# Where the latent queries and keys of an attention layer are split into two parts: at each load, or once where they are made

## The chip, the cores and the metric

The kernel runs on one core of one Trainium2 chip. The metric is the device time of one execution in microseconds (us). A core has a matrix engine (PE, with its weight loads shown as PEld), a vector engine (DVE), a scalar engine (ACT), a third elementwise engine (POOL) and a queue engine (SP) that issues most transfers between on-chip memory and DRAM. Each engine works through its own instructions in order.

## The reference, cut to what matters

Two layers of a decoder trunk with 1024 tokens of width 1024. The change touches the first layer's latent attention: eight heads, each with a query and key of 64 elements made from a normalised low-rank vector, and 32 rotary elements; the rotary part of the key is shared by all heads.

```python
q = (rmsnorm(z_cq, q_norm) @ w_uq).reshape(b, s, MLA_HEADS, MLA_NOPE + MLA_ROPE)
q_nope = q[..., :MLA_NOPE]
q_rope = apply_rope(q[..., MLA_NOPE:], cos_r, sin_r)
kv = (rmsnorm(z_ckv, kv_norm) @ w_ukv).reshape(b, s, MLA_HEADS, MLA_NOPE + MLA_V)
k_nope = kv[..., :MLA_NOPE]
k_rope = apply_rope(z_kr[:, :, None, :], cos_r, sin_r)[:, :, 0, :]
...
s = jnp.einsum('bqhd,bkhd->bhqk', qn, k_nope) + jnp.einsum('bqhr,bkr->bhqk', qr, k_rope)
s = jnp.where(causal_block_mask(blk, seq), s.astype(jnp.float32) * scale, NEG_INF)
p = jax.nn.softmax(s, axis=-1).astype(v.dtype)
return jnp.einsum('bhqk,bkhd->bqhd', p, v)
```

## The kernel before, in words

Everything is held with features on the 128 partitions and tokens along the free dimension, in two chunks of C = 512 tokens. To keep precision, each matrix operand is held as two tiles of a reduced float format: `hi`, a rounded copy, and `lo`, what is left. `split` (line 89) makes them: ACT copies the source to `hi` (L91), DVE or POOL subtracts to get `lo` (L92). A product is three matmuls: hi by hi, hi by lo, lo by hi (L127, L128 and L130 in projections, L441 in scores).

The work of the first layer comes in stages.

1. The first projections, and a list of "first" jobs built in `even_first` (line 660). It ends with the jobs that the change touches: `kr` makes the rotary key of a chunk and stores it to the DRAM tensor `krd` (L693); `qrope` evicts the two halves of the rotary query (L702), rotates them (L707 to L712) and stores them to `qrd` (L713, L714); `v` evicts latent values (ACT, L726); and `to` evicts latent queries and keys, four pairs of heads by query and key by chunk, with a multiplication on DVE (L720) and stores them to `qd` and `kd` (L721). All evicted blocks go to tiles with the tag `t`, a ring of eight tiles of 128 by 512. The latent vectors that these jobs read lie in the ring of twenty `qk` tiles, which they fill entirely.
2. Beside these jobs, `ada_behind` (line 312) loads modulation weights (L281) and sums them on DVE (L283), a step at a time.
3. Latent attention in `latent_items` (line 769), with window attention joined in towards its end. For each head and chunk `load_latent` (line 750) is called one head and chunk ahead. It issues five transfers on SP (L763) into one of two wide tiles of tag `x8` (the profile calls it `x`): 64 rows of query, two lots of 16 rows of rotary query, 64 rows of key and 32 of rotary key. Then it splits query and key into four tiles of the `qk` ring. This happens sixteen times.
4. `weave` (line 1124) merges attention with a filling of further projections, which need weights from the `wr` ring (loads L107, splits on ACT and POOL) and stores their results; its merge by costs gives the order in which the program is written. A planner then fixes each engine's order before the run, by that order as priority and by its own estimates of when inputs and free tiles are there. A tile that is not free makes the instruction that would write it wait, and with it what stands behind it on its engine.

SP issues its transfers in order: weights, modulation weights, stores, loads of the attention, and the small transfers that turn softmax sums into rows (L479, L491).

Of the kernel before, what the change touches and what calls it, by code (L numbers as in the profile page):

```python
# [10 lines left out]
F32 = mybir.dt.float32  # L11
F32R = mybir.dt.float32r
# [10 lines left out]
C = 512  # L23
# [10 lines left out]
class Trunk:  # L34
# [4 lines left out]
    def __init__(self, ctx, tc, I, out):  # L39
        self.tc, self.nc, self.I, self.out = tc, tc.nc, I, out  # L40
        self.ctx = ctx
        self.sb = ctx.enter_context(tc.tile_pool(name="sb", bufs=1))
        self.ps = ctx.enter_context(tc.tile_pool(name="ps", bufs=1, space=PSUM))
        self.dr = ctx.enter_context(tc.tile_pool(name="dr", bufs=1, space=DRAM))
        self.sb2 = None
        self.BUFS = dict(self.BUFS)
        self.n = 0
        d = lambda name, shape: self.dr.tile(shape, F32, name=name, tag=name)
        self.x1d = d("x1d", [2, 128, 8, C])
        self.ogd = d("ogd", [2, 8, 2, 128, C])  # L50
        self.gd = d("gd", [8, 2, 128, C])
        self.qd = d("qd", [4, 128, 1024])
        self.qrd = d("qrd", [2, 128, 1024])
        self.kd = d("kd", [4, 128, 1024])
        self.krd = d("krd", [32, 1024])
        self.vd = d("vd", [5, 2, 128, C])
        self.wd = d("wd", [5, 2, 128, C])
        self.fd = d("fd", [8, 1024])
        self.rd = d("rd", [2, 8, 2, 2, C])
# [600 lines left out]
    def even_first(self, h, tables):  # L660

        nc, I = self.nc, self.I
# [4 lines left out]
        def keep(i, n, g, dst, rs, col=None):  # L667
# [13 lines left out]
                    return lambda: rs.__setitem__(ch, self.copied(self.rstd(sq[n, ch], 128 * n, col and col[:, 4 * ch:4 * ch + 4]), self.t("g", [128, C])))  # L681
            return use

        def kr(ch, p):
            cs = slice(ch * C, ch * C + C)
            a, b, mk = self.tmp(), self.tmp(), self.tmp()
            nc.sync.dma_start(mk, I["mk"][:, cs])
            nc.vector.tensor_tensor(out=a, in0=p, in1=mk, op=ALU.mult)
            nc.sync.dma_start(b[0:64], a[64:128])
            nc.gpsimd.tensor_tensor(out=a[0:64], in0=a[0:64], in1=b[0:64], op=ALU.add)  # L690
            nc.sync.dma_start(mk[0:32], a[32:64])
            nc.gpsimd.tensor_tensor(out=a[0:32], in0=a[0:32], in1=mk[0:32], op=ALU.add)
            nc.sync.dma_start(self.krd[:, cs], a[0:32])  # L693

        half = {}

        def qrope(w):
            def use(ch, p):
                mc, ms = tables
                cs = slice(ch * C, ch * C + C)  # L700
                t = self.tmp()
                nc.vector.tensor_tensor(out=t, in0=p, in1=rq[ch], op=ALU.mult)  # L702
                half[w, ch] = t
                if w == 1:
                    za, zb = half[0, ch], t
                    t0, t1 = self.tmp(), self.tmp()
                    nc.vector.tensor_tensor(out=t0, in0=za, in1=ms[:, cs], op=ALU.mult)  # L707
                    nc.gpsimd.tensor_tensor(out=t1, in0=zb, in1=ms[:, cs], op=ALU.mult)
                    nc.vector.tensor_tensor(out=za, in0=za, in1=mc[:, cs], op=ALU.mult)
                    nc.gpsimd.tensor_tensor(out=zb, in0=zb, in1=mc[:, cs], op=ALU.mult)  # L710
                    nc.vector.tensor_tensor(out=za, in0=za, in1=t1, op=ALU.subtract)
                    nc.vector.tensor_tensor(out=zb, in0=zb, in1=t0, op=ALU.add)  # L712
                    nc.sync.dma_start(self.qrd[0, :, cs], za)  # L713
                    nc.sync.dma_start(self.qrd[1, :, cs], zb)  # L714
            return use

        def to(d, r):
            def use(ch, p):
                z = self.tmp()
                nc.vector.tensor_tensor(out=z, in0=p, in1=r[ch], op=ALU.mult)  # L720
                nc.sync.dma_start(d[:, ch * C:ch * C + C], z)  # L721
            return use

        def v(ch, p, b):
# [6 lines left out]
        hh = {0: h[0], 1: h[1]}  # L731
        full = lambda n, use: (w[n], 8, 128, [(0, 8, hh, use)])
        jobs = [full(10 + i, keep(i, 3, self.v_qn, cn, rq)) for i in range(3)]
        jobs += [full(13 + i, keep(i, 2, self.v_kvn, kn, rk, rkc)) for i in range(2)]
        jobs += [self.gate_job(h, 15, 0), (I["wkr"], 8, 128, [(0, 8, hh, kr)]), self.gate_job(h, 16, 1)]
        cc, kk = {0: cn[0], 1: cn[1]}, {0: kn[0], 1: kn[1]}
        jobs += [(I["wqr"], 6, 128, [(3 * i, 3, cc, qrope(i)) for i in range(2)])]
# [12 lines left out]
    def load_latent(self, u, hh, c):  # L750

        nc = self.nc
        hd = 2 * u + hh
        cs = slice(c * C, c * C + C)
        out = []
        both = self.t("x8", [128, 1024])
        for n, parts in enumerate(([(0, 64, self.qd[u, 64 * hh:64 * hh + 64, cs])] +
                      [(64 + 16 * e, 80 + 16 * e, self.qrd[e, 16 * hd:16 * hd + 16, cs]) for e in range(2)],
                      [(0, 64, self.kd[u, 64 * hh:64 * hh + 64, cs]), (64, 96, self.krd[:, cs])])):
            raw = both[:, n * C:n * C + C]  # L760
            hi, lo = (t[:96] for t in self.hl("qk"))
            for a, b, d in parts:
                nc.sync.dma_start(raw[a:b], d)  # L763
            self.split(hi, lo, raw[:96])
            out.append((hi, lo))
        (qh, ql), (kh, kl) = out
        return (qh, ql, qh), (kh, kh, kl)

# [673 lines left out]
```

## Time and profile before

| what | value |
|---|---|
| median of three runs | 1367.68 us (1365.36 to 1367.77) |
| the profiled execution | 1368.67 us, of which the span of instructions is 1366.9 us |
| PE busy | 1269.7 us (93%) |
| DVE busy | 912.3 us (67%) |
| ACT busy | 734.4 us (54%) |
| POOL busy | 352.5 us (26%) |
| transfers | 173.85 MB, 127 GB/s over the span |
| clock granted to PE | 0.987 of full speed over the span |

Busy time is from one profiled execution; matmuls are pipelined, so a matmul of 512 columns that is shown with 0.39 us starts 0.23 us after the one before it where nothing holds it up. In rows of the order of time the first number is the start in us, the second the duration, and a bracket at the end holds the engine's idle time before it and what ended it. Rows by tile give the least, median and greatest duration in ns. Tile names stand without their numbers, and `out<-in` says what is written from what.

### The profile page before, as it was taken

The numbers are of one execution on the slowest core, as the hardware profiler recorded it, in microseconds if no ns is written. First come the engines' busy times: TensorE is split into PE (matmuls) and PEld (weight loads), VectorE is DVE, ScalarE is ACT, GpSimd is POOL, SyncE is SP. The second block draws the span as 40 slices with busy tenths as digits, with TensorE's granted clock in tenths as the row PEclk, the third lists the DMA queues.
The fourth block names the chain that finished last, engine by engine and source line by source line (L and its number), as shares of the span: only waits on it lengthen the run. The fifth ranks groups of instructions, "written<-read, shape, count | busy, mean of one in ns | idle before, by whom it ended". The sixth has DMA issues, their size and how long they took to land.

```text
span 1366.9 us, 20727 instructions
## 1 busy us (share of the span) xinstructions
PE 1269.7 (93%) x6876; PEld 1055.4 (77%) x6876; DVE 912.3 (67%) x2058; ACT 734.4 (54%) x1515; POOL 352.5 (26%) x324
## 2 busy tenths in 40 slices
PE   2899999999999999999979999999999999999996
PEld 1678778888777777777757878787888888887896
DVE  6855757777668785787866776667646564656475
ACT  4253226555558577765545554447545455556542
POOL 2243421331233215300003322321222212233400
PEclk9999999999999999999999999999999999999998
DMA  8606685555354444373533222212112121233283
GB/s 284 249 19 210 194 277 189 170 161 178 109 158 138 156 124 138 103 231 123 176 92 104 70 59 66 49 56 76 52 38 78 54 78 55 85 117 103 78 270 121
DMA packets 103723, 173.85 MB, mean 127 GB/s; under 512 B 16304, under 2 KB 25520, under 8 KB 103616
## 3 DMA queue, kind: packets, MB, share of 16 engines
q1 hardware_dynamic: 99104, 169.91, 38.9%
q10 hardware_dynamic: 4512, 2.62, 0.6%
q8 instruction: 54, 0.88, 0.3%
q14 instruction: 53, 0.43, 0.1%
HBM read 129.36 MB, written 31.72 MB: 118 GB/s over the span
## 4 chain that ended last, share of the span: by engine, by line
PE 42%; DVE 12%; ACT 6%; issue 5%; DMA 5%; POOL 1%; SPq 1%; POOLq 0%; DVEq 0%; ACTq 0%
PE pj L127 8%; PE pj L128 8%; PE pj L130 8%; PE S L441 6%; PE pt L501 3%; PE o L511 2%; DVE pt_l L92 1%; DVE p L463 1%; DMA wr<-in_wout_dram 1%; PE o L510 1%; ACT wh L91 1%; PE S L127 1%; PE S L130 1%; PE S L128 1%; DMA t<-wd 1%
## 5 line engine op out<-in xcount | busy, mean ns | idle before, releaser
L127 PE MATMUL pj<-h,wh 128*128 128x512 f32 (+1 forms) x816 | 338.9, 416 | 1.5 <-ACT wh L91 1.5
L128 PE MATMUL pj<-h,wh 128*128 128x512 f32 (+1 forms) x816 | 322.2, 395 | 0.0
L130 PE MATMUL pj<-h,wl 128*128 128x512 f32 (+1 forms) x800 | 316.0, 395 | 2.2 <-DVE wl L92 2.2
L92 POOL TENSOR_TENSOR wl<-wr,wh 128x512 fp32r<-128x512 f32 x126 | 166.4, 1330 | 461.5 <-ACT wh L91 428.9
L466 ACT ACTIVATE p<-p,sm 128x128 f32<-128x128 f32 (+3 forms) x192 | 148.8, 775 | 146.8 <-DVE sm L463 143.0
L92 DVE TENSOR_TENSOR pt_l<-pt,pt_h 128x512 fp32r<-128x512 f32 (+1 forms) x232 | 146.9, 635 | 99.4 <-ACT pt_h L91 97.5
L441 PE MATMUL S<-qk,qk 96*128 96x512 f32 (+5 forms) x720 | 175.3, 344 | 20.6 <-DVE sm L463 11.4
L130 PEld LDWEIGHTS pj<-h,wl 128*128 128x128 f32 x800 | 151.0, 189 | 35.0 <-DVE wl L92 3.8
L91 ACT ACTIVATE pt_h<-pt 128x512 fp32r<-128x512 f32 (+1 forms) x232 | 127.6, 552 | 89.3 <-PE pt L501 87.5
L127 PEld LDWEIGHTS pj<-h,wh 128*128 128x128 f32 (+1 forms) x816 | 153.9, 189 | 20.3 <-ACT wh L91 2.3
L441 PEld LDWEIGHTS S<-qk,qk 128*128 128x128 f32 (+1 forms) x720 | 120.2, 188 | 63.2 <-DVE sm L463 25.5
L128 PEld LDWEIGHTS pj<-h,wh 128*128 128x128 f32 (+1 forms) x816 | 154.4, 189 | 17.1 <-DVE h L92 0.2
L91 ACT ACTIVATE wh<-wr 128x512 fp32r<-128x512 f32 x165 | 100.9, 622 | 115.4 <-PE S L128 38.6
L501 PE MATMUL pt<-ident,p 128*128 128x128 f32 x840 | 134.3, 274 | 3.1 <-DVE p L945 3.1
L501 PEld LDWEIGHTS pt<-ident,p 128*128 128x128 f32 x840 | 101.5, 140 | 26.1 <-DVE p L945 4.4
L463 DVE CUSTOM_DVE_ANT_0 p<-S,mask 128x640 f32<-128x640 f32 (+7 forms) x128 | 96.0, 750 | 35.0 <-PE S L441 34.1
L510 PE MATMUL o<-pt_h,v 128*128 128x256 f32 (+1 forms) x408 | 106.3, 279 | 2.1 <-ACT pt_h L91 1.7
L511 PE MATMUL o<-pt_l,v 128*128 128x256 f32 (+1 forms) x408 | 102.3, 285 | 5.6 <-DVE pt_l L92 5.3
L348 POOL TENSOR_TENSOR t<-t,rs 128x512 f32<-128x512 f32 x26 | 36.8, 1414 | 229.0 <-DMA t<-t 147.4
L511 PEld LDWEIGHTS o<-pt_l,v 128*128 128x128 f32 x408 | 77.2, 189 | 16.6 <-DVE pt_l L92 11.2
L510 PEld LDWEIGHTS o<-pt_h,v 128*128 128x128 f32 x408 | 77.0, 189 | 11.2 <-ACT pt_h L91 4.8
L127 PE MATMUL S<-h,wh 128*128 128x512 f32 (+1 forms) x144 | 57.5, 399 | 3.9 <-ACT h L332 2.7
(317 smaller groups left out, 2288.6 us busy)
## 6 DMA issues: line engine op xcount, KB each, us to landing
wr<-in_wod_dram SPq DMA_DIRECT2D x80, 256.0 KB
wr<-in_wout_dram SPq DMA_DIRECT2D x68, 256.0 KB
ad<-in_wadab_dram SPq DMA_DIRECT2D x41, 256.0 KB
wr<-in_wev_dram SPq DMA_DIRECT2D x38, 256.0 KB
raw<-in_wadaa_dram SPq DMA_DIRECT2D x32, 256.0 KB
ogd<-t SPq DMA_DIRECT2D x32, 256.0 KB
t<-t SPq DMA_DIRECT2D x106, 64.0 KB
t<-rd SPq DMA_DIRECT2D x48, 128.0 KB
```

Of the source, the lines that this page charges most:

```text
L91: nc.scalar.activation(hi, src, AF.Copy)
L92: (lo_eng or nc.vector).tensor_tensor(out=lo, in0=src, in1=hi.bitcast(F32), op=ALU.subtract)
L127: nc.tensor.matmul(p, w[0][:, k, :m], h[0], start=first, stop=False)
L128: nc.tensor.matmul(p, w[0][:, k, :m], h[1], start=False, stop=last and w[1] is None)
L130: nc.tensor.matmul(p, w[1][:, k, :m], h[0], start=False, stop=last)
L348: nc.gpsimd.tensor_tensor(out=s, in0=s, in1=self.rs[:, cs], op=ALU.mult)
L441: nc.tensor.matmul(dst, a, k[:, s], start=(n == 0), stop=n == len(q) - 1)
L463: nc.vector.tensor_tensor_reduce(out=P[:, s], in0=S[:, s], in1=a, scale=-scale, scalar=init, op0=ALU.add, op1=ALU.min, accum_out=nm)
L466: nc.scalar.activation(P[:, :n], P[:, :n], AF.Exp, bias=nm, scale=-1.0, accum_out=l)
L501: nc.tensor.transpose(pt[:, n * 128:n * 128 + 128], b, self.ident)
L510: nc.tensor.matmul(o[:, qcols], w, hi[:, cols], start=start, stop=False)
L511: nc.tensor.matmul(o[:, qcols], w, lo[:, cols], start=False, stop=stop)
```

## The change

Each latent query and key block is split where it has just been made. `keep_split` takes a new `t` tile for `hi`, writes `lo` over the block itself, and stores both, so the four DRAM tensors get a dimension of two. `load_latent` no longer uses the `x8` tile and splits nothing: for `hi` and `lo` of query and key it issues ten transfers straight into the four `qk` tiles.

```diff
-        self.qd = d("qd", [4, 128, 1024])
-        self.qrd = d("qrd", [2, 128, 1024])
-        self.kd = d("kd", [4, 128, 1024])
-        self.krd = d("krd", [32, 1024])
+        self.qd = d("qd", [4, 2, 128, 1024])
+        self.qrd = d("qrd", [2, 2, 128, 1024])
+        self.kd = d("kd", [4, 2, 128, 1024])
+        self.krd = d("krd", [2, 32, 1024])
...
+        def keep_split(z, d, cs):
+            hi = self.t("t", [128, C], F32R)[:z.shape[0]]
+            lo = z.bitcast(F32R)
+            self.split(hi, lo, z)
+            for n, x in enumerate((hi, lo)):
+                nc.sync.dma_start(d[n, :, cs], x.bitcast(F32))
...
-            nc.sync.dma_start(self.krd[:, cs], a[0:32])
+            keep_split(a[0:32], self.krd, cs)
...
-                    nc.sync.dma_start(self.qrd[0, :, cs], za)
-                    nc.sync.dma_start(self.qrd[1, :, cs], zb)
+                    keep_split(za, self.qrd[0], cs)
+                    keep_split(zb, self.qrd[1], cs)
...
                 nc.vector.tensor_tensor(out=z, in0=p, in1=r[ch], op=ALU.mult)
-                nc.sync.dma_start(d[:, ch * C:ch * C + C], z)
+                keep_split(z, d, slice(ch * C, ch * C + C))
...
-        both = self.t("x8", [128, 1024])
-        for n, parts in enumerate(([(0, 64, self.qd[u, 64 * hh:64 * hh + 64, cs])] +
-                      [(64 + 16 * e, 80 + 16 * e, self.qrd[e, 16 * hd:16 * hd + 16, cs]) for e in range(2)],
-                      [(0, 64, self.kd[u, 64 * hh:64 * hh + 64, cs]), (64, 96, self.krd[:, cs])])):
-            raw = both[:, n * C:n * C + C]
-            hi, lo = (t[:96] for t in self.hl("qk"))
-            for a, b, d in parts:
-                nc.sync.dma_start(raw[a:b], d)
-            self.split(hi, lo, raw[:96])
-            out.append((hi, lo))
+        for parts in ([(0, 64, self.qd[u, :, 64 * hh:64 * hh + 64, cs])] +
+                      [(64 + 16 * e, 80 + 16 * e, self.qrd[e, :, 16 * hd:16 * hd + 16, cs]) for e in range(2)],
+                      [(0, 64, self.kd[u, :, 64 * hh:64 * hh + 64, cs]), (64, 96, self.krd[:, :, cs])]):
+            both = tuple(t[:96] for t in self.hl("qk"))
+            for n, t in enumerate(both):
+                for a, b, d in parts:
+                    nc.sync.dma_start(t[a:b].bitcast(F32), d[n])
+            out.append(both)
```

## The prediction

> **What bounds the kernel now.** I read the page first: its shares of busy time, then the slices.
>
> ```profile
> PE 1269.7 (93%) x6876; PEld 1055.4 (77%) x6876; DVE 912.3 (67%) x2058; ACT 734.4 (54%) x1515; POOL 352.5 (26%) x324
> ```
>
> PE is the bound over the whole span: 97 of 1366.9 us are left as gaps. The change touches two stages: the projections that make latent queries and keys, and the latent attention that reads them back. So the table by stretches comes next; its columns are PE, PEld, DVE, ACT and POOL busy time with the number of instructions, the clock, the DMA share and GB/s.
>
> ```profile
> 150.00:174.00 24.00, 21.63 (x97) 17.28 (x96) 18.37 (x23) 5.32 (x9) 10.61 (x8) 1.00 0.62 195
> 174.00:202.00 28.00, 26.86 (x123) 21.72 (x121) 16.98 (x27) 6.29 (x12) 4.88 (x4) 1.00 0.83 274
> 202.00:350.00 148.00, 144.43 (x818) 121.24 (x818) 106.67 (x212) 91.22 (x194) 38.66 (x45) 1.00 0.56 176
> 350.00:460.00 110.00, 103.67 (x604) 86.30 (x603) 79.79 (x185) 68.54 (x167) 33.80 (x35) 1.00 0.42 131
> 175.00:180.00 5.00, 3.85 (x17) 2.84 (x16) 3.25 (x5) 0.61 (x2) 1.45 (x2) 1.00 1.06 333
> ```
>
> From 150 to 174 us rotary queries and latent values are made, from 174 to 202 us the sixteen blocks of latent queries and keys (PE 96% busy, DMA 0.83 busy), and from 202 us on attention runs with projections as filling. In attention PE idles 148 - 144.4 = 3.6 us before 350 us and 110 - 103.7 = 6.3 us up to 460 us: 9.9 us is the most that lighter DVE and ACT can give back to PE's gaps there. The last row, the busiest five microseconds of DMA in this stage, gives the most that was moved, 333 GB/s.
>
> What ends PE's gaps in attention is in the view of the waits, for 202 to 460 us:
>
> ```profile
> PE S L441 <- DVE sm L463: 4.2, 7, 1.2
> PE o L511 <- DVE pt_l L92: 3.1, 4, 1.4
> ```
>
> DVE ends most of them, so DVE work taken out of attention is worth something. In the projections the gaps have two other makers, seen in the order of time:
>
> ```profile
> 162.59 0.69 ACT L726 ACTIVATE t<-S,rkc 128x512 f32<-128x512 f32 x1 [8.52 <-DVE t L712]
> 163.33 0.50 PE L140 MATMUL S<-wh,qk 128*128 128x512 f32 x1 [2.37 <-ACT t L726]
> 178.10 0.75 DVE L283 SCALAR_TENSOR_TENSOR ad<-ad,sc 128x512 f32<-128x512 f32 x1 [0.75 <-DMA ad<-in_wadab_dram]
> 178.77 0.68 DVE L720 TENSOR_TENSOR t<-S,g 128x512 f32<-128x512 f32 x1
> 179.51 0.50 PE L127 MATMUL S<-qk,p 128*128 128x512 f32 x1 [1.15 <-DVE t L720]
> ```
>
> At 162.6 us ACT had waited 8.5 us for one of the eight "t" tiles, and PE lost 2.4 us behind it. At 178 us DVE, in order, waited for a landing of the modulation weights (L283); the eviction L720 stood behind it, and PE lost 1.15 us. Both the "t" tiles and the landings are what the change asks more of.
>
> **The change part by part.** Rows for the prices (duration is least, median and most, in ns; the row of a stretch is here of instructions on "qk" tiles alone, where DVE's and ACT's are the four splits):
>
> ```profile
> L91 ACT ACTIVATE qk<-x x32: 615/622/634, 195.5 to 450.5; 96x512 fp32r<-96x512 f32 x32
> L92 DVE TENSOR_TENSOR qk<-x,qk x32: 675/687/1517, 196.1 to 452.3; 96x512 fp32r<-96x512 f32 x32
> L763 SPq DMA_DIRECT2D x<-qd x16: 450/451/590, 185.0 to 352.0; - x16
> L763 SPq DMA_DIRECT2D x<-qrd x32: 307/504/1579, 170.1 to 354.5; - x32
> L763 SPq DMA_DIRECT2D x<-krd x16: 303/582/1552, 165.7 to 359.1; - x16
> L721 SPq DMA_DIRECT2D qd<-t x8: 319/367/790, 176.0 to 201.3; - x8
> 174.00:202.00 28.00, 26.21 (x114) 20.75 (x112) 2.65 (x4) 2.53 (x4) 0.00 (x0) 1.00 0.83 274
> L92 DVE TENSOR_TENSOR qk<-x,qk 96x512 fp32r<-96x512 f32 x23 | 18.2, 794 | 3.8 <-ACT qk L91 3.8
> 450.32 1.43 DVE qk L92
> 452.42 0.73 DVE qk L92
> 418.64 0.74 DVE qk L92
> 395.81 3.32 DMA t<-wd
> L283 DVE SCALAR_TENSOR_TENSOR ad<-ad,sc 128x512 f32<-128x512 f32 x6 | 4.5, 752 | 4.8 <-DMA ad<-in_wadab_dram 4.2 <-ACT ad L286 0.6
> ```
>
> *Removed from the attention loads:* 32 ACT copies of 0.622 us (19.9 us) and 32 DVE subtracts of 0.687 us median (22 us, somewhat more by the slow ones). From 202 to 350 us that is 18.2 of DVE's 106.7 us, a sixth. PE's gaps there are 3.6 us, so a sixth is 0.6 us and all of them the upper end. In the next stretch three of the subtracts stand on the chain that ended last, 1.43 + 0.73 + 0.74 = 2.9 us. Gain taken: 0.6 + 2.9 = 3.5 us; bounds 0 (what follows on the chain is as late) and 9.9 us.
>
> *Added where queries and keys are made:* 22 copies and 22 subtracts (16 blocks from L720, four rotary query halves, two rotary keys), priced by the same rows at 13.7 us of ACT and 15.1 us of DVE. The two rotary key blocks fall near 140 us:
>
> ```profile
> 140.68 0.34 SPq L693 DMA_DIRECT2D krd<-t  x1
> 140.00:145.00 5.00, 4.62 (x22) 3.53 (x21) 3.33 (x4) 0.60 (x1) 1.93 (x2) 1.00 0.57 142
> ```
>
> PE has 0.4 us of gaps there, DVE and ACT have room, and nobody reads the rotary key before attention; taken at 0, at most 2 x 1.31 = 2.6 us if that cover were gone.
>
> *150 to 174 us:* four copies and four subtracts, 2.75 us more on a DVE that is busy 18.4 of 24 us, and four more "t" tiles in the ring that already kept ACT and PE waiting. Bounds 0 (the released tile of L712 comes ahead of the new work) and 2.75 us (all subtracts ahead of the evictions). The first chunk's two subtracts stand ahead of the second chunk's eviction L702, the other two do not: I take 2 x 0.687 = 1.4 us.
>
> *174 to 202 us:* DVE goes from 16.98 to 16.98 - 2.65 + 16 x 0.687 = 25.3 us, ACT from 6.29 to 6.29 - 2.53 + 16 x 0.622 = 13.7 us. With the 4.8 us that DVE waits ahead of the six L283 the stage needs 30.1 us of DVE in 28: 2.1 us over. DMA moved 28 us x 274 GB/s = 7.7 MB; sixteen more stores of 256 KB are 4.2 MB and the doubled loads of the first heads about 0.8 MB (five of 128 KB, three of 32 and one of 64 KB are issued in it): 12.7 MB, at 333 GB/s 38 us, 10 us more than the stage has. What can slip is the modulation weights (six of 256 KB) and three weight loads for the filling, 2.4 MB or 7.1 us; 2.9 us stay. They add to the DVE term, because a later landing lengthens DVE's wait ahead of L283, with the evictions behind it. Taken 2.1 + 2.9 = 5.0 us; bounds 0 (the filling takes PE's place in every gap) and 10 us (DMA sets the pace). The ring bounds this too: each block now holds two of eight "t" tiles through copy, subtract, store and landing.
>
> The Trainium skill, "DMA: Bandwidth & Descriptors", section Specifications, gives about 358 GB/s as HBM's limit for a core. By that figure the 12.7 MB would be an estimated 35.4 us, the same slip would leave about 0.8 us, and the sum below would be 2.1 us lower; the trace does not show more than 333 GB/s at a share of 1.06 here, and that is used.
>
> *The first load of attention:* before, raw data lay ready and the split started when the projections' tiles came free; after, the transfers themselves wait for these tiles.
>
> ```profile
> 188.56 0.62 ACT L91 ACTIVATE wh<-wr 128x512 fp32r<-128x512 f32 x1
> 195.48 2.71 ACT L91 ACTIVATE qk<-x 96x512 fp32r<-96x512 f32 x4 [6.31 <-PE S L128]
> 201.70 0.45 PE L441 MATMUL S<-qk,qk 96*128 96x128 f32 x3
> 201.98 0.44 PE L127 MATMUL pj<-h,wh 128*128 128x512 f32 x1
> ```
>
> Ten transfers take 4 x 0.45 + 4 x 0.50 + 2 x 0.58 = 5.0 us of SP and 3.3 us to land (the row of a 64-row load of "wd"): 195.5 + 8.3 = 203.8, 2.1 us after the first score. The filling's matmul stands right behind that score, but PE is in order. Bounds 0 and 2.1; I take 1.0.
>
> *SP in attention:* 80 more transfers in all, about 65 of them after 202 us, 32 us. From the first to the second row here it issued some 190 transfers in about 92 of 148 us:
>
> ```profile
> 202.99 0.95 SPq L656 DMA_DIRECT2D t<-vd  x2
> 347.36 0.32 SPq L649 DMA_DIRECT2D g<-gd  x1
> 417.37 0.62 ACT L91 ACTIVATE qk<-x 96x512 fp32r<-96x512 f32 x1
> 454.29 1.24 PE L441 MATMUL S<-qk,qk 96*128 96x512 f32 x6
> ```
>
> So it goes to some 124 of 148 us, in order, with waits for "qk" tiles now on SP in place of ACT. Queued behind such a wait are the filling's weights (L107), the window's loads and the rows of the softmax sums. I cost it at 0, since two thirds of the time SP had slack of its own and loads are issued a head ahead; bounds -0.5 and +12 (a third of 32 us comes through to PE's weights). The late loads have room: by the order of the heads what was split at 417 us was first read by the scores at 454 us.
>
> **Sum.** 1.4 + 5.0 + 1.0 - 3.5 = +3.9 us on the profiled execution's 1368.67 us (span 1366.9): 1372.6 us. The median of the three runs is 1367.68, 1.0 lower, so for runs **1371.6 us**, slower by 0.29%. About 0.2%, 2.7 us, is what a measurement of this kernel can tell from no change.
>
> **Rivals.** *Relief wins (faster).* The filling covers every new gap before 202 us, and the 3.5 us stay: 1364.2 us, at best 1357.8 with all 9.9. For it: the weights of the first filling job were copied at 188.6 us, ahead of need, and DVE ends PE's waits in attention. Against: the DVE and DMA sums above, both over the stage's length. It decides if PE's gaps from 150 to 202 us stay at their 3.5 us.
>
> *Hidden to hidden (no change).* The splits at the loads cost nothing, since PE was 98% busy over them, and where they go PE is 96% busy too; the change then does not do what it is meant to: 1367.7 us. The row of PE's 144.43 us speaks for it, the chain's three subtracts against.
>
> *SP runs dry (clearly slower).* With 124 of 148 us and waits for tiles in its queue, weights come late again and again: 3.9 and about 8 of the 12 us above give 1380 us. The 63% of now speaks against. It decides when SP's idle time ahead of L763 (on "qk" tiles) adds up to more than its remaining 24 us. The same page of the Trainium skill, section "Issuing engines are not separate DMA queues", calls issue time usually small beside the transfer; 0.45 us beside 3.32 agrees for one load, but not for the queue's total.
>
> **How the numbers follow.** Forecast 40%, relief 30%, hidden 18%, SP dry 12%. The forecast's own range is 1368 (all terms at zero) to 1378 (the terms of 150 and 174 us at their upper ends, 2.75 and 10 us: 6.4 us more). For 8 in 10 the range reaches from most of the relief case to the SP case: 1360 to 1382. Of the forecast's chance 70% lies above 0.2%, 25% within and 5% below; of relief's 75% is faster and 25% within; of hidden's 70% is within and 15% on either side; all of SP's is slower. Faster: 0.27. Within 0.2%: 0.30. Slower: 0.43.
>
> **What would show it.** Right: copies and subtracts of "qk" from "x" are gone; DVE above 24 us busy and DMA share above 0.95 from 174 to 202 us; more PE gaps ended by DVE L720 or by "t" tiles before 202 us; the first score some 5 us later; fewer gaps from 350 to 460 us. Wrong: if the projections end as early as before, the DMA and DVE terms fall; if gaps in attention grow, ended by weights (ACT wh) or by "qk" landings, it is SP. The instruction order on each engine can also come out otherwise than the rows of before suggest, since the planner fixes it anew from the changed work; no row of before shows that, and it is in the range.

## The result, and the profile after

The changed kernel takes 1429.74 us (median of four runs, 1427.63 to 1430.04), beside 1367.13 us for the kernel before on the same chip. The ratio is 1.0449, with a 95% interval from 1.0431 to 1.0466: about 62 us slower, where 4 were forecast and 1382 us was the upper end. Its profiled span is 1425.9 us. The page's busy times after:

```profile
PE 1293.4 (91%) x6876; PEld 1070.3 (75%) x6876; DVE 906.2 (64%) x2048; ACT 731.2 (51%) x1505; POOL 351.4 (25%) x324
```

PE runs the same 6876 matmuls but is busy 23.7 us longer, and its gaps grow from 97 to 132.5 us; the two together are the 59 us of span. DVE and ACT, which were to be relieved in one stage and loaded in another, do slightly less in all. The table by stretches after (columns as in the prediction):

```profile
150.00:174.00 24.00, 18.81 (x79) 14.26 (x77) 19.49 (x24) 4.49 (x9) 12.46 (x10) 0.93 0.52 167
174.00:202.00 28.00, 23.90 (x99) 18.59 (x100) 15.53 (x24) 11.90 (x21) 5.08 (x4) 0.88 0.80 270
202.00:350.00 148.00, 134.83 (x696) 110.53 (x695) 82.06 (x165) 67.41 (x142) 30.13 (x33) 0.96 0.53 169
350.00:460.00 110.00, 94.08 (x510) 79.10 (x511) 58.53 (x115) 50.80 (x108) 27.68 (x33) 0.92 0.58 172
460.00:510.00 50.00, 42.97 (x225) 35.28 (x225) 31.75 (x100) 30.20 (x85) 9.90 (x11) 0.86 0.49 152
```

The same clock times now hold fewer matmuls (79 for 97, 99 for 123, 696 for 818), and PE's clock, the third number from the right of each row, falls below 1.00 where before it was 1.00 throughout. Counting matmuls in stretches of 10 us in both traces, and comparing the times at which equal numbers have been run, gives where the time goes: the changed kernel is 10 us late where the one before stands at 189 us, 15 at 220, 31 at 322, 33 from 373 to 400, 47 at 428 and 55 at 455, and stays 53 to 56 late to the end. So about 15 us are lost where queries and keys are made, about 16 in the first half of the latent attention, and about 22 near its end. The 16 us were not followed to single causes: from 202 to 350 us PE's gaps grow from 3.6 to 13.2 us with no wait longer than 1.8 us, and the clock is 0.96.

The waits of PE after, for 150 to 235 us and then for 235 to 510 us (what waited, what ended it: us in total, times, longest):

```profile
PE S L140 <- ACT t L733: 5.0, 2, 4.2
PE pj L140 <- DVE t L709: 3.3, 1, 3.3
...
PE pj L127 <- ACT t L343: 12.3, 1, 12.3
PE pt L295 <- DVE ad L283: 9.4, 3, 6.1
PE o L511 <- DVE pt_l L92: 4.4, 7, 1.6
PE S L441 <- DVE sm L463: 2.4, 5, 0.9
```

Two waits of 4.2 and 3.3 us fall among the latent values, behind evictions of ACT and DVE. In the attention a wait of 12.3 us stands out, behind ACT's eviction of a rope job (L343), and one of 6.1 us behind DVE's sum of modulation weights (L283). The order of time tells how the first came about. SP's queue, then ACT:

```profile
433.40 1.27 SPq L479 DMA_DIRECT2D rd<-t  x4
...
435.15 0.45 SPq L769 DMA_DIRECT2D qk<-qd  x1
...
440.10 0.58 SPq L769 DMA_DIRECT2D qk<-krd  x1
...
442.14 1.14 SPq L107 DMA_DIRECT2D wr<-in_wev_dram  x2
...
443.90 5.51 SPq L806 DMA_DIRECT2D t<-wd  x8
```

```profile
446.75 0.63 ACT L91 ACTIVATE wh<-wr 128x512 fp32r<-128x512 f32 x1 [5.61 <-DMA wr<-in_wev_dram]
...
450.11 0.63 ACT L808 ACTIVATE qk<-t 128x512 fp32r<-128x512 f32 x1 [1.78 <-DMA t<-wd]
...
453.72 0.63 ACT L808 ACTIVATE qk<-t 128x512 fp32r<-128x512 f32 x1 [0.72 <-DMA t<-wd]
...
455.48 0.57 ACT L343 ACTIVATE t<-pj 128x512 f32<-128x512 f32 x1
```

From 435.15 to 440.68 us SP issues one block's ten loads. Behind them stand the next weights (L107) and the eight loads of the window's queries and keys (L806). ACT waits in order 5.6 us for the weights and then for four of the window loads; the eviction L343, which PE waits for, comes behind them. In the kernel before the eight window loads were issued at 395.28 us with no block's load near them (the last of them starts at 359.1 us, in the prediction's rows), ACT had copied weights at 391.4 and 392.4 us without a wait, and its L343 came at 404.91 us among other work, with no wait of PE. What the stall did to the DMA and to PE's clock, in the stretches of after and then in PE's rows:

```profile
440.00:445.00 5.00, 3.79 (x21) 2.94 (x19) 1.40 (x2) 0.59 (x1) 0.00 (x0) 1.00 0.77 250
445.00:450.00 5.00, 0.00 (x0) 0.00 (x0) 1.00 (x2) 1.26 (x2) 2.48 (x2) 0.70 1.02 281
450.00:455.00 5.00, 0.00 (x0) 0.00 (x0) 3.22 (x5) 3.17 (x7) 0.26 (x1) 0.50 1.05 270
```

```profile
456.11 0.80 PE L127 MATMUL pj<-h,wh 128*128 128x512 f32 x1 [12.32 <-ACT t L343]
456.70 0.63 PE L128 MATMUL pj<-h,wh 128*128 128x512 f32 x1
...
460.88 0.40 PE L127 MATMUL pj<-h,wh 128*128 128x512 f32 x1
```

For ten microseconds the DMA engines are full (shares 1.02 and 1.05) with what SP issued in one go, while PE does nothing. PE's granted clock falls to half during the gap, and a matmul of 512 columns takes 0.63 to 0.80 us in place of 0.40 until 460.6 us, 4.5 us after PE started again. The Trainium skill, "TensorE: Matmul & The Clock Gate", Part 1, says that about 3.4 us without work halves the clock and about 3.4 us of work give it back. The trace is near that here: 0.70 over 445 to 450 us means half clock for three of the five, from about 447 us on, some 3.2 us after PE's last matmul ended (443.8 us), and the return took 4.5 us. At the next stall it isn't, and the measurement decides: there the clock is halved from about 481.2 us, 2.0 us after the last matmul, until 494.7 us, 9.5 us after PE started again.

That next stall, the wait of 6.1 us, has the same maker, a block's ten loads, with less between. SP, DVE and PE after:

```profile
475.99 0.48 SPq L769 DMA_DIRECT2D qk<-qd  x1
...
480.89 0.58 SPq L769 DMA_DIRECT2D qk<-krd  x1
481.52 0.42 SPq L281 DMA_DIRECT2D ad<-in_wadab_dram  x1
```

```profile
484.35 0.75 DVE L283 SCALAR_TENSOR_TENSOR ad<-ad,sc 128x512 f32<-128x512 f32 x1 [9.02 <-DMA ad<-in_wadab_dram]
485.25 1.84 PE L295 MATMUL pt<-ones,ad 128*128 128x1 f32 x8 [6.07 <-DVE ad L283]
490.00:495.00 5.00, 5.00 (x23) 4.81 (x23) 4.08 (x12) 4.24 (x10) 0.18 (x2) 0.52 0.48 171
```

The load of modulation weights (L281) stands right behind the ten loads, DVE has waited 9.0 us when it lands, and PE waits for DVE. In the kernel before the matmul L295 of this place, at 423.33 us, has no wait. The two stalls fit the two steps of the count, from 33 to 47 and from 47 to 55 us.

SP does not stand longer in all. Its waits from 200 to 530 us, of the kernel before and then after:

```profile
SPq L479 <- DVE t L476: 42.1, 22, 5.2
...
SPq L1236 <- DVE t L349: 11.2, 7, 2.8
```

```profile
SPq L1241 <- DVE t L349: 37.7, 8, 8.9
SPq L479 <- DVE t L476: 23.6, 13, 6.3
...
SPq L769 <- PE S L441: 1.6, 4, 0.6
```

It stands 37.7 us at the stores of the ropes (L1236 before, L1241 after) where it stood 11.2, and less elsewhere, at L479 above all: its waits in this stretch add up to 112 us, before to 140. What has changed is where it stands and what has gathered behind. At the loads themselves it hardly waits: the ten longest rows of L769 make 9.6 us, of which PE's release of "qk" tiles is 1.6.

### The profile page after: what moved, and what is told of

It is laid out like the page before. It is cut to its first block, busy times and chain, and to the rows that moved or that the text cites. A ratio compares the mean times of both kernels' runs of the same rounds, so it can differ in the third digit from the quotient of the medians.

```text
span 1425.9 us, 20870 instructions
## 1 busy us (share of the span) xinstructions
PE 1293.4 (91%) x6876; PEld 1070.3 (75%) x6876; DVE 906.2 (64%) x2048; ACT 731.2 (51%) x1505; POOL 351.4 (25%) x324
## 4 chain that ended last, share of the span: by engine, by line
PE 35%; DVE 9%; issue 4%; ACT 4%; DMA 3%; POOL 0%; SPq 0%; POOLq 0%; DVEq 0%; ACTq 0%
PE pj L127 7%; PE pj L128 7%; PE pj L130 7%; PE S L441 4%; PE pt L501 3%; DMA wr<-in_wout_dram 2%; PE o L511 1%; DVE p L463 1%; PE o L510 1%; DVE qk L399 1%; ACT wh L91 1%; PE S L127 1%; PE S L130 1%; PE S L128 1%; DMA wr<-in_wod_dram 1%
## 5 line engine op out<-in xcount | busy, mean ns | idle before, releaser
L127 PE MATMUL pj<-h,wh 128*128 128x512 f32 (+1 forms) x816 | 336.7, 413 | 15.9 <-ACT t L343 12.3
L441 PE MATMUL S<-qk,qk 96*128 96x512 f32 (+5 forms) x720 | 181.7, 347 | 22.2 <-DVE sm L463 12.2
L127 PEld LDWEIGHTS pj<-h,wh 128*128 128x128 f32 (+1 forms) x816 | 154.0, 189 | 38.9 <-ACT t L343 12.7
L501 PE MATMUL pt<-ident,p 128*128 128x128 f32 x840 | 139.5, 282 | 4.0 <-DVE p L950 3.8
L463 DVE CUSTOM_DVE_ANT_0 p<-S,mask 128x640 f32<-128x640 f32 (+7 forms) x128 | 96.2, 751 | 67.4 <-PE S L441 64.4
L510 PE MATMUL o<-pt_h,v 128*128 128x256 f32 (+1 forms) x408 | 112.1, 291 | 1.8 <-DVE t L550 0.8
L511 PE MATMUL o<-pt_l,v 128*128 128x256 f32 (+1 forms) x408 | 107.1, 295 | 7.2 <-DVE pt_l L92 6.7
```

Of the source, the lines that this page charges most:

```text
L127: nc.tensor.matmul(p, w[0][:, k, :m], h[0], start=first, stop=False)
L441: nc.tensor.matmul(dst, a, k[:, s], start=(n == 0), stop=n == len(q) - 1)
L463: nc.vector.tensor_tensor_reduce(out=P[:, s], in0=S[:, s], in1=a, scale=-scale, scalar=init, op0=ALU.add, op1=ALU.min, accum_out=nm)
L501: nc.tensor.transpose(pt[:, n * 128:n * 128 + 128], b, self.ident)
L510: nc.tensor.matmul(o[:, qcols], w, hi[:, cols], start=start, stop=False)
L511: nc.tensor.matmul(o[:, qcols], w, lo[:, cols], start=False, stop=stop)
```

## The experiments

All ratios are against runs of the kernel before on the same chip; "us" after a plus sign is the ratio times 1367. The first four runs asked which side of the change costs, and whether it is the number of transfers on SP, the places they wait for, or the making side.

| run | what differs | median us | ratio, 95% interval |
|---|---|---|---|
| m_only | making side alone | 1387.43 | 1.0152, 1.0085 to 1.0219 |
| l_only | load side alone, ten loads | 1407.98 | 1.0302, 1.0233 to 1.0371 |
| b_twice | before, each load in two halves | 1372.56 | 1.0053, 1.0023 to 1.0083 |
| a_pool | change, five of ten loads on GpSimd | 1385.26 | 1.0136, 1.0084 to 1.0188 |
| l_five | five raw loads straight into place, split there | 1370.14 | 1.0028, 1.0010 to 1.0045 |
| l_pool | load side, five of ten on GpSimd | 1377.65 | 1.0087, 1.0069 to 1.0105 |
| l_pair | load side, five loads of double size | 1401.08 | 1.0233, 1.0198 to 1.0268 |
| l_ten | l_five and five more loads | 1406.44 | 1.0290, 1.0269 to 1.0311 |
| l_small | l_five and five more loads of 16 columns | 1388.43 | 1.0171, 1.0148 to 1.0194 |
| l_early | load side, loads at higher priority | 1410.87 | 1.0323, 1.0299 to 1.0346 |
| a_pair | change, five loads of double size | 1433.40 | 1.0462, 1.0426 to 1.0498 |
| a_early | change, loads at higher priority | 1442.50 | 1.0560, 1.0526 to 1.0594 |
| m_noqr | making side, rotated queries unsplit | 1373.40 | 1.0056, 1.0039 to 1.0073 |
| m_dve | making side, their hi rounded by DVE | 1382.75 | 1.0125, 1.0109 to 1.0141 |
| m_pth | making side, hi not in "t" tiles | 1390.01 | 1.0142, 1.0112 to 1.0172 |
| best2 | a_pair and m_pth | 1426.37 | 1.0410, 1.0378 to 1.0442 |
| best3 | a_early and m_pth | 1420.52 | 1.0392, 1.0364 to 1.0419 |
| two_queues | change, lo stores and loads on GpSimd, m_pth | 1386.35 | 1.0152, 1.0129 to 1.0175 |

**The sides, apart.** m_only keeps `keep_split` and loads only the high part, as the kernel before loads (five transfers to "x8", then the split); l_only keeps the unsplit DRAM tensors and reads the block into both places:

```diff
# l_only
+            both = tuple(t[:96] for t in self.hl("qk"))
+            for n, t in enumerate(both):
+                for a, b, d in parts:
+                    nc.sync.dma_start(t[a:b].bitcast(F32), d)
```

> The making side of the change alone: every latent query and key block is split where it is made and both parts are stored, but the attention loads only the hi part, with the five transfers of before, and splits it again as before (the lo part that it then subtracts is nearly nothing, so the output is less precise). Theory SP (the doubled transfers of the loads fill the issuing queue, and what stands behind them comes late): the loss up to the end of the projections stays, the loss in attention goes, so about 1367 + 14 = 1381 us, range 1376 to 1388. Theory MAKING (tile ring, DVE and DMA at the projections, and a start that is upset by them for good): at least 1410 us. Theory TILES (transfers hold or wait for qk tiles): as SP, about 1381 us.

> The load side of the change alone: the blocks are stored once and unsplit as before, and the attention loads each of them twice, straight into the tiles of hi and of lo, with ten transfers and no split (so the unsplit block stands in both places and the output is wrong by that). Theory SP: the loss in attention comes back without that of the making, 1367 + 30 to 48 us, about 1407 us. Theory MAKING: within 8 us of before. Theory TILES: about 1407 us, as SP.

About +21 and +41 us: the sides add up to the change's 62, as far as two runs of each tell (12 to 30 and 32 to 51 us). At equal numbers of matmuls m_only is 10 us late at 189 us and 16 at 270, and loses nothing after; l_only loses nothing before 270 us, is 13 late at 400 and 34 at 455, with waits of PE of 12.2 us for ACT's L343 and 6.0 us for L283 as in the change; some 7 us more are lost between 510 and 950 us, which was not followed.

**Number of transfers alone.** b_twice is the kernel before with each of the five loads cut into two halves of the columns, so ten transfers of the same bytes into "x8"; a_pool is the change with `(nc.gpsimd if n else nc.sync).dma_start(...)`, the five loads of the low part on GpSimd's queue.

> The kernel before, with each of the five transfers of a load issued as two halves of 256 columns: ten transfers for each head and chunk, the bytes, tiles and splits of before. Theory SP: most of the loss in attention without any other part of the change, 1390 to 1415 us. Theory TILES and a theory of bytes (the DMA engines have too much to move): within 5 us of before, 1362 to 1373 us. Theory MAKING: the same.

> The changed kernel, with the five transfers for lo issued from POOL's queue and the five for hi from SP: SP issues as many transfers in the attention as before. Theory SP: the loss in attention goes for the most part, 1380 to 1395 us, unless POOL's own work (its splits of weights) comes late by the transfers. Theory TILES and the theory of bytes: within 8 us of the changed kernel, 1422 to 1438 us. Theory MAKING: the same.

Ten transfers for five into the staging tile cost 7 us. With half of them on GpSimd's queue, the same bytes and places, the change costs no more than its making side alone (+19 beside +21), and PE's waits for L343 and L295 are gone from the trace. The Trainium skill, "DMA: Bandwidth & Descriptors", section Issuing engines are not separate DMA queues, has it that a second issuing engine saves only issue time, usually small; here it saved 43 us. SP's order changed with it: the eight window loads are issued at 413.88 us, and the last load of a block ahead of them at 374.11 us. So the saving goes with what stands behind what on SP; the issue time alone was not parted from it.

**Late loads, few or many.** l_five takes the staging tile away but keeps the split; l_pool is l_only with a_pool's edit.

```diff
# l_five
+            hi, lo = (t[:96] for t in self.hl("qk"))
+            for a, b, d in parts:
+                nc.sync.dma_start(lo[a:b].bitcast(F32), d)
+            self.split(hi, lo, lo.bitcast(F32))
```

> The five raw loads of the kernel before go straight into the place of the low part, with no staging block ahead of it; ACT and DVE split from there as in the kernel before. Theory A (the block of ten on SP): five loads as late as in the change, but half as many, cost a small part, 1367 to 1380 us. Theory C (what costs is that a load can't run ahead because it waits for its place among the 20 tiles, and SP stands at it whatever the number): most of the 42 us is there, 1395 us or more.

> The load side alone (the unsplit block is read into both places, so the low part is not the low part), with the second place's five loads issued from GpSimd's queue. Theory A (ten loads that become free to run together are a block of 5.3 us on the in-order SP queue, and window loads, ada loads and stores stand behind it): with half of the block gone from SP the 42 us of the load side alone are gone, 1362 to 1374 us, no wait of PE over 6 us, and since ACT and DVE are rid of the splits it may come out a few us under the kernel before. Theory B (the two sides interact: GpSimd's queue helps only because the making side had moved the plan): 1385 us or more.

Five loads that wait for their places cost 4 us, so waiting for places (theory C) is not it. In this run, though, no block's load stands on SP between 359 and 429 us, and the window loads are issued at 399 us: the planner had kept the order of the kernel before, so five loads right ahead of the window's were not tried. l_pool came out 4 us above its range: +12, of which 9 are lost between 244 and 296 us by the count of matmuls, with PE's longest waits there for DVE's L463 (3.2 and 2.4 us); what makes them was not followed further. So the second queue does not take the whole load side away by itself, and a_pool's +19 is not the sum of +21 and +12.

**Size in place of number.** a_pair and l_pair put both parts side by side into one tile of 1024 columns and fetch each piece by one transfer (in l_pair the unsplit piece, twice). The "qk" ring becomes ten such tiles, which come free in pairs only, so the waiting for places changes too. The lines of a_pair:

```diff
+            pair = self.t("qk", [128, 2, C], F32R)
+            both = pair[:96, 0], pair[:96, 1]
+            for a, b, d in parts:
+                nc.sync.dma_start(pair[a:b].bitcast(F32), d.rearrange("n p c -> p n c"))
```

> The whole change, but high and low part lie side by side in one tile of 1024 columns (ten such tiles in place of twenty), and each of the five pieces is fetched with one transfer for both parts: five loads a block instead of ten, the same bytes, just as late. Theory A (the block of ten late loads on SP): the load side's 42 us are gone and only the making side's 16 to 20 us are left, 1378 to 1390 us. If bytes or the waiting for tiles cost what the ten loads cost: 1405 us or more.

> The load side alone (the unsplit block is read into both places), each piece fetched into both places by one transfer: five late loads a block, no staging block, no split on ACT and VectorE in the attention. Theory A: 1364 to 1372 us; beside the five late loads with the split kept (1370 us) it shows what the splits taken out of ACT and VectorE are worth. If the relief that the prediction counted (3.5 us) is there: 1362 to 1367 us. If not: 1368 to 1372 us. If bytes cost: 1385 us or more.

Theory A, as I had put it, fell: five transfers of double size cost 63 and 32 us, about what ten cost. Both have the long wait of PE behind the same rope eviction (10.0 and 9.0 us). So the number alone is not it; left are the bytes on SP's queue, the order that the planner makes of them, or the missing splits.

**Splits kept, second loads large or small.** l_ten issues the five raw loads of l_five also into the high part's place, which ACT then overwrites; l_small does it for 16 of 512 columns.

```diff
# l_ten
+                for t in (hi, lo):
+                    nc.sync.dma_start(t[a:b].bitcast(F32), d)
# l_small
+                nc.sync.dma_start(hi[a:b, :16].bitcast(F32), d[:, :16])
+                nc.sync.dma_start(lo[a:b].bitcast(F32), d)
```

> The five raw loads go straight into the place of the low part, and the same five also into the place of the high part; ACT and VectorE then split over them as in the kernel before. Ten late transfers, twice the bytes, and nothing is taken from ACT and VectorE: beside the five late loads (1370 us) only the second five are new. Theory P (twice the bytes on SP's queue make the planner that orders the instructions put the blocks' loads two to three blocks later in SP's order, among window loads, weights and ropes, and SP stands there in order): 1398 to 1415 us, with the 9 to 12 us wait of PE for the rope's eviction. Theory R (the loss comes of the missing splits: PE hangs on the loads themselves): 1368 to 1378 us.

> As the ten late loads with the split kept (1406 us), but the second five fetch 16 of 512 columns only: 3% more bytes than five loads instead of 100%, and ACT writes over them. The order in which SP's transfers stand among ropes, weights, gates and window loads is as good as that of the ten full loads. Theory P (the order costs the time): 1397 to 1412 us, with the same long wait of PE for the rope's eviction near 430 us. Bytes, on the chip or on SP's ring: 1368 to 1380 us.

l_ten at +40 shows that the missing splits have no part in it (theory R fell). l_small missed both ranges: +23, in the middle. PE's waits from 202 to 510 us of l_small and of l_ten:

```profile
PE pt L295 <- DVE ad L283: 7.1, 2, 5.9
...
PE pj L127 <- ACT t L343: 4.0, 1, 4.0
```

```profile
PE pj L127 <- ACT t L343: 11.6, 1, 11.6
PE pt L295 <- DVE ad L283: 9.5, 3, 5.9
```

The stretches of l_small and of l_ten in which PE stands for L343:

```profile
410.00:415.00 5.00, 1.38 (x9) 0.86 (x7) 4.88 (x6) 4.06 (x9) 2.06 (x3) 0.96 0.83 255
```

```profile
425.00:430.00 5.00, 0.00 (x0) 0.00 (x0) 0.67 (x1) 1.26 (x2) 2.17 (x2) 0.68 1.01 286
430.00:435.00 5.00, 0.00 (x0) 0.00 (x0) 3.60 (x5) 3.13 (x6) 0.73 (x2) 0.50 1.02 277
```

In both the order of time on SP has a block's ten loads just ahead of the weights and the window's loads (from 394 us in l_small, from 416 us in l_ten), with the same transfers in between, and both stall at L343 and at L283. The stall at L283 is 5.9 us in both: there the places are enough, without the second loads' bytes. Without the second loads' bytes the stall at L343 is 4.0 us in place of 11.6, and SP's standing at the rope stores (L1235) is 10.3 us in place of 28.9. So of the 36 us between l_five and l_ten some 20 come with the second five loads' places in the queue and some 16 with their bytes. How much of the bytes' part is the full DMA of that moment (1.01 and 1.02, beside 0.83), and how much SP's later arrival at it, these runs don't part.

The traces of the other runs bear on that order. From 235 us on the long waits for L343 and L283 are in the change, l_only, l_ten and l_small, and in a_pair and l_pair by their own line numbers; in each of them SP issues a whole block in the last 9 us ahead of the window loads. In l_five, l_pool, a_pool and two_queues there is no wait for either, and SP issues no block's load in the 30 us ahead of the window loads. b_twice shows that the block alone is not enough: its ten loads go from 389.39 to 396.62 us, window loads follow at 399.75 us, and neither wait is there. But part of the weights stands ahead of this block (379.28 and 380.70 us), and the DMA share of 395 to 400 us is 0.34.

**The order alone.** l_early and a_early put the loads under a higher priority (600), so that they stand earlier on SP.

> The load side alone, with the same ten transfers, bytes, queue and tiles, but issued at a higher priority (600 steps earlier for the planner), so that they stand ahead of the stage's window loads and weights in SP's order, as in the kernel before. Theory P: most of the 42 us goes, 1365 to 1382 us, and SP's waits at the rope stores fall from 36 us to under 20. If bytes or the number on the chip cost what was lost: 1400 us or more.

> The whole change with the loads' higher priority alone. Theory P: the load side's part goes and the making side's 16 to 20 us stay, 1380 to 1397 us; if early loads also let the first scores start earlier, 1375 us. If the bytes are the cause: 1420 us or more.

Both expectations failed. In l_early the wait at L343 near 430 us is gone, as foreseen, but others come before it: 10.9 us of PE at 234 us for an ACT eviction (L367), 5.1 and 5.2 us near 340 us. SP's waits in it:

```profile
SPq L1235 <- DVE t L349: 23.6, 7, 9.6
SPq L763 <- PE S L441: 16.4, 10, 4.7
```

Issued early, the loads now do wait for PE to release "qk" tiles, 16.4 us on SP, with everything else behind them. The longest wait has another reason, seen on SP and on ACT:

```profile
230.97 0.35 SPq L721 DMA_DIRECT2D kd<-t  x1
```

```profile
233.42 0.60 ACT L367 ACTIVATE t<-pj 128x512 f32<-128x512 f32 x1 [9.26 <-DMA kd<-t]
```

From 205 to 230.9 us SP issues loads of blocks one after another, with 1.1 us of waits; the stores of keys (L721) stand behind them, a "t" tile is not free until one has landed, and ACT waits 9.3 us for it, and PE 10.9 us for ACT. So earlier is not better in this kernel: on a queue that runs in order the early loads hold back the stores.

**The making side.** In m_noqr the rotated queries are stored unsplit; in m_dve ACT's part of their split is given to DVE; in m_pth the high part lies in the tiles "pt_h" and "pt_l", which are idle until the attention, not in one of the eight "t" tiles.

> The making side alone (loads of the high part only, split after the load as in the kernel before), but the rotated queries are stored in one part, unsplit; latent queries, keys and the rotated key are still split where they are made. Theory D (ACT stands in order at the splits of the rotated queries, which end a chain over GpSimd and VectorE, and the evictions of the values, which free PE's PSUM, stand behind them): the gap of PE ahead of the value matmuls and the halved clock after it go, and of the 16 to 20 us of the making side at most 6 stay, 1367 to 1374 us. Theory E (doubled stores and the ring of eight temporaries): one part in eleven of the splits is left out, 1382 us or more.

> The making side alone, with all its splits, but the high part of the rotated queries is rounded by VectorE instead of ACT: four VectorE operations of about 0.7 us more, four ACT operations fewer. Theory D (ACT stands in order): most of the 16 to 20 us goes, 1368 to 1376 us, and the waits of PE for ACT at the value evictions are under 2 us. Theory E (temporaries and stores): 1382 us or more, since the same temporaries are held and the same bytes stored. If VectorE is the bound of this stage: 1387 us or more.

> The making side alone, with all its splits on ACT and VectorE and all its stores, but the rounded high part lies in the buffers that the attention uses later for its transposed weights (pt_h and pt_l, four in all) and no longer takes a place in the ring of eight temporaries t. Theory F (the high parts fill the ring of temporaries, and the evictions that free PE's PSUM wait for a free one): 1367 to 1375 us, no wait of PE over 2.5 us at 160 to 180 us, no halved clock there. Theory D (the splits stand in order ahead of the evictions on ACT and VectorE): as the making side alone, 1380 us or more.

Four splits of 22 left out, with their four tiles and four stores (m_noqr), take 13 of the 21 us away. What they do is seen from 164 to 184 us, in m_only, m_noqr and m_pth:

```profile
164.00:184.00 20.00, 11.86 (x27) 8.41 (x28) 13.91 (x20) 6.09 (x10) 3.25 (x2) 0.57 0.79 259
```

```profile
164.00:184.00 20.00, 17.63 (x67) 13.10 (x67) 13.16 (x17) 7.15 (x13) 4.39 (x4) 0.91 0.83 259
```

```profile
164.00:184.00 20.00, 17.65 (x72) 13.67 (x72) 12.72 (x19) 8.96 (x16) 3.03 (x2) 0.91 0.87 272
```

In m_only PE loses two waits (3.3 us for DVE's L709, 4.0 us for ACT's L733) and runs at 0.57 of its clock: 27 matmuls in 20 us, where the kernel before ran 87. m_dve keeps a 3.3 and a 2.9 us wait, and +17 us, though ACT splits no rotated query there, so it is not ACT's part of these splits (theory D). With the high part out of the "t" ring (m_pth) PE's waits there are 1.7 us for DVE and 2.3 us for modulation weights, and the clock stays at 0.91, so the ring has a part in them (theory F). But the total stays, +19 where theory F gave 8 at most: PE then stands for the first attention block, which SP fetches from 210 us on, behind all 32 stores of queries and keys, and the clock of 210 to 236 us is 0.67 (before 1.00). From PE's waits of m_pth, 150 to 235 us:

```profile
PE S L442 <- ACT qk L91: 5.1, 1, 5.1
```

**Together.**

> The whole change with both mendings: one transfer for both parts into a tile of 1024 columns, and the rounded high part in the buffers pt_h and pt_l while it is stored. Theories A and F together: 1364 to 1375 us, as the kernel before or a little under it. If F falls: 1378 to 1390 us.

> The whole change with the loads' higher priority, and the rounded high part in the buffers pt_h and pt_l while it is stored. With the buffers alone the making side's stalls at 160 to 180 us were gone but PE stood 5.1 us for the first attention load, which stood on SP behind the 32 stores; with the loads ahead in the order that wait should go too: 1366 to 1380 us if both theories hold, 1385 us or more if the making side's cost is in its stores and splits themselves.

> The whole change with the low parts on GpSimd's queue both ways (stores where they are made, loads in the attention) and the rounded high part in the buffers pt_h and pt_l. SP then has the number of transfers of the kernel before, and the order of its stores, first loads, weights and ropes is close to that kernel's. If the making side's 18 us come of SP's order and of the ring of temporaries, as the load side's come of SP's order: 1364 to 1376 us. If they come of the splits on ACT and VectorE: 1380 us or more. GpSimd's own wait at the loads of the load side alone cost 11 us in an earlier run; if that is added again, 1376 to 1382 us.

None beats the kernel before. best2 loses 56 us where a_pair loses 63, and best3 54 where a_early loses 77: beside the early loads the high part in "pt_h" and "pt_l" gives back 23 us, why was not followed. two_queues, with SP's number of transfers as before and the ring relieved, still takes 21 us more. PE's waits from 150 to 235 us, and a stretch:

```profile
PE S L442 <- DMA qk<-krd: 5.3, 2, 3.3
PE pj L141 <- DVE t L711: 2.5, 1, 2.5
```

```profile
184.00:210.00 26.00, 23.71 (x107) 19.03 (x107) 22.77 (x35) 10.92 (x19) 13.83 (x22) 1.00 1.02 370
```

From 184 to 210 us the DMA is full, 370 GB/s at a share of 1.02, and the first attention loads land late. So the making side's 20 us have no single cause that these runs take away: when the ring of temporaries is relieved, PE's longest wait moves to the first attention block behind SP's doubled stores, and when half of those leave SP, to that block's landing behind a full DMA. That is what the waits show; the share of each is open. No run keeps the doubled stores and leaves out the splits' work on ACT and DVE, so that work stays a rival.

## Why the prediction was wrong

*Direction and relief.* Slower was right; the size, 4 us against 62, was not, and the range ended 48 us short of the median. The relief of 3.5 us is not found, nor can it be excluded. The nearest pair are l_only, without splits in the attention (+32 to +51 us), and l_ten, which keeps them (+37 to +42); l_five, with all its splits, is the fastest of the load side's versions.

*SP in attention, the step that failed.* It was costed at 0 with bounds of -0.5 and +12; it is worth about 41 us (l_only), two thirds of the result. The reasoning was one of sums: SP goes from 92 to 124 of 148 us, so it has slack. SP did keep slack: it issued for some 100 of these 148 us, and its waits from 200 to 530 us fell from 140 to 112 us. What counted was what stands behind what on a queue that runs in order: the window's loads and weights behind a block of ten, ACT's evictions behind these, PE behind the eviction (12.3 us), and at the second stall the modulation weights behind a block of ten, DVE behind these, PE behind DVE (6.1 us). The kernel before had the same queue without these waits; its loads, into a staging tile, were all out by 359 us. The shares of places and bytes in the 41 us are known only from l_small and l_ten, some 20 and 16, and the losses before 350 us were not followed to their waits.

*SP runs dry.* This rival named the right engine and the right victims ("weights come late"; ACT's 5.6 us for "wr"), with a wrong point of decision. It was to show as SP idle for more than 24 us ahead of the "qk" loads; that was 9.6 us. It gave 1380 us, some 12 over the kernel before, where the load side alone cost 41. The late loads "have room", the forecast said of the scores that read them; what stands behind them in the queue had none.

*150 to 174 us (+1.4, bounds to 2.75) and 174 to 202 us (+5.0, bounds to 10).* Together measured at about 15 us by the change's count of matmuls at 220 us, and 21 us by m_only. The sign and the maker were right for the first: PE's new waits end at L709 and at ACT's L733, the "t" tiles. The size was not: 7.5 us of waits (4.2 and 3.3), and a clock of 0.93 and 0.88 after them. For the second the mechanism was wrong. DVE was to pass 24 us and the DMA share 0.95; they show 15.53 us and 0.80 in this stretch, since PE had come late and with it the work. The ceiling of 333 GB/s was also misread: it is the most of stretches that start at full fives, and the trace of before shows more in the same stage:

```profile
178.00:183.00 5.00, 3.85 (x17) 2.88 (x16) 2.78 (x5) 0.00 (x0) 0.00 (x0) 1.00 1.05 376
```

At 376 GB/s the forecast's own sum, 12.7 MB less 2.4, is an estimated 27.4 us in a stage of 28, and its DMA term of 2.9 us is nothing.

*The first load (+1.0, bounds to 2.1).* The first score starts at 226.14 us in place of 201.70, 24 us later in place of 5:

```profile
226.14 0.43 PE L441 MATMUL S<-qk,qk 96*128 96x128 f32 x2 [1.49 <-DMA qk<-krd]
```

Only 1.5 us of it are PE's wait for the landing, inside the bounds; the rest is the stage before it and the filling that PE ran instead. The forecast let the ten loads start when their places came free; on SP they also stood behind the doubled stores, and all but the first were issued from 220.17 us on.

*What had no term at all.* First, the half clock after a wait: in each stretch of the table from 150 to 510 us the clock was 1.00 and is 0.86 to 0.96, and over the span PE is busy 23.7 us longer for the same matmuls. A forecast that adds up waits alone leaves this out. Second, the planner's new order: the forecast named it in its last sentence and put it "in the range", but no width of the range came from it.

## What to carry to other kernels

Before a transfer is moved or doubled on an in-order queue, list what will stand behind it at the moment it becomes free to run, and who waits for that; the sum of issue times against the span says nothing about it. A staging tile that looks like a useless copy can be what lets a queue run ahead, and the same bytes can cost 12 us with half the loads on a second queue where from the first alone they cost 41 (l_pool and l_only). On a kernel that keeps PE 93% busy, price a wait of PE of 3 us or more at its length and again a few us for the clock that it takes away: after the waits of 12.3 and 6.1 us PE worked 4.5 and 9.5 us at half clock.

## What the chip showed that was not expected

A wait of 3.3 us was enough to bring PE's clock down, and a second one of 4 us some 4 us later kept it there: 0.57 over the 20 us around both (m_only). It stayed halved until 183 us, 9 us after PE had started again, though PE was busy for 7.9 of these. Shorter waits can be followed by it too: in the changed kernel one of 1.8 us, at 347 us, was followed by half clock until about 355 us, while the 2.4 us at 163 us of the kernel before left its clock at 1.00. The DMA engines moved 370 GB/s over 26 us with stores and loads mixed (two_queues); the kernel before shows 393 GB/s over five microseconds, from 30 to 35 us at a share of 1.05.
